# Three moves in the last five tiles of a top-10 kernel: stores to another queue, copy steps one tile earlier, one ranking later

## The chip, the cores and the metric

The kernel runs on one core of one Trainium2 chip. Its time is the device time of one execution in microseconds (us); the number given for a kernel is the median of several executions. The profile is one execution recorded by the hardware profiler. Its engines are PE (TensorE, the matmuls, with PEld for the loading of weights), DVE (VectorE), ACT (ScalarE), POOL (GpSimd) and SP (SyncE). ACTq and SPq are the sequencers of ACT and SP, which issue DMA transfers.

## The reference

The input is a random matrix of 8192 rows and 8192 columns in float32. For each row the reference returns the column numbers of the ten largest values, largest first, as int64:

```python
def reference(x, k):                      # k = 10
    indices = np.argpartition(x, -k, axis=1)[:, -k:]
    values = np.take_along_axis(x, indices, axis=1)
    sorted_idx = np.argsort(-values, axis=1)
    return np.take_along_axis(indices, sorted_idx, axis=1)
```

## The kernel before

**Tiles and batches.** The rows are worked through in 64 tiles of 128 rows (4 MB of input each). The variable `t` counts tiles from 0 to 63, and `last` is 63. Results are finished and stored in batches. Batches 0 to 6 hold eight tiles each (batch 6: tiles 48 to 55), batch 7 holds five (56 to 60) and batch 8 holds three (61 to 63).

**The work on a tile.** A tile goes through these steps, each named after its function in the listing.

- `load` (L88): SP issues the transfers that bring the tile into one of four buffers. They are 1 MB each, four a tile; the first and the last tile have eight pieces of 512 KB.
- `weigh` (L138): ACT takes the exponential of the tile (L144) into one of three buffers `e`, and PE adds groups of columns up into 1024 sums per row, `s` in PSUM (L152). It runs in two halves, in tile 63 in five parts of 2, 2, 2, 1 and 1 eighths. An eighth of tile 63 is one piece of the load.
- `choose_steps` (L157): DVE finds the 12 best of the 1024 sums, with six instructions (L171 to L177). The last of them writes the list `idx`.
- `gather` (L183): POOL fetches the values of the chosen groups by that list (L185), into `cand`.
- `spread` (L195): the fetched values are multiplied by a mask (L203) into `masked`. Half of the 12 groups are done by DVE and half by POOL. For tile 61 POOL does all 12; for tile 63 DVE does 8.
- `extract` (L210): 12 float32 matmuls (recorded as 24 instructions, L214) bring the values into their rows' order, into `g` in PSUM. The pool of `g`, `gpsum`, has three buffers (L72).
- `rank_steps` (L217): DVE sorts out the ten best of the 96 values, with six small instructions (L225 to L231). The first three of them that work on values (L225, L226, L228) read `g`; the others don't.
- `finish_steps` (L236): for a whole batch, DVE turns the places found into column numbers (`slot`, `low`, `hot`, `hot` again, `pick`, `val`, `rows`: L257 to L272), PE brings them into output order with one `move` per tile of the batch (L252, two recorded instructions each) into the single PSUM buffer `fo`, DVE copies `fo` to `opack` (L276), and a transfer stores `opack` (L278). That list has seven DVE steps, the moves, the copy and the store, in this order: 17 steps for a batch of eight.

**The order.** All of it stands under `tc.manual_schedule()`: each engine issues its instructions in the order in which the code below emits them, and an engine that waits holds up all that stands behind it. Waits between engines, and for a buffer that is still being read, are put in by the framework. The main loop (L296) emits for tile `t`: `choose(t)` interleaved with `rank(t-3)`, `spread(t-1)`, `gather(t)`, `weigh(t+1)`, `extract(t-1)`, some steps of the pending batch, and `load(t+3)`. The pending batch's steps wait in the list `later`; `todo` of them are emitted per tile, 3 as a rule and 6 from tile 59 on (L304). The 17 steps of batch 6 enter the list at tile 58. So they are emitted as 6 at tile 59 (to `val`), 6 at tile 60 (`rows` and five moves) and 5 at tile 61 (three moves, the copy, the store). Those of tile 61 stand behind `weigh(62)` and ahead of `choose(62)` and `weigh(63)`. Each store is issued by ACT's sequencer.

After the loop (L312 to L339) come `choose(63)` and the last spreads, extracts and ranks, with the steps of batch 7 put in between by hand, and then batch 8. A short check of the whole result follows, which ends in a value that all engines read (L348) before the program ends.

Of the kernel before, what the change touches and what calls it, by code (L numbers as in the profile page):

```python
# [14 lines left out]
S = P // A  # L15
# [4 lines left out]
TB = 8  # L20
# [5 lines left out]
LAG = 3  # L26
# [4 lines left out]
def kernel(  # L31
# [6 lines left out]
    nc = tc.nc  # L38
# [19 lines left out]
    out_rows = out_u32.rearrange("(r a) n -> r (a n)", a=A)  # L58
# [20 lines left out]
    last = ntiles - 1  # L79

    starts = list(range(0, ntiles, TB)) + [last - 2]
# [35 lines left out]
    for s in range(S):  # L117
        nc.vector.tensor_copy(
            out=group[:, s, :].rearrange("p (a s) -> p a s", s=S)[:, :, s], in_=own_a
# [37 lines left out]
    def choose_steps(t):  # L157
        m = ss.pop(t)
        b = batch_of[t]
        i = t - starts[b]  # L160
        if i == 0:
            batch[b] = (
                cpool.tile([P, TB, 16], u16, tag="cidb", name="cidb"),
                cpool.tile([P, TB, 16], u16, tag="posb", name="posb"),
            )
        cid = batch[b][0][:, i, :]
        w16 = wall[:, t, :]
        m2 = small.tile([P, W], fp32, tag="m2", name="m2")
        idxs[t] = small.tile([P, G], u16, tag="idx", name="idx")
        return [  # L170
            lambda: nc.vector.max(out=w16[:, 0:8], in_=m),  # L171
            lambda: nc.vector.match_replace(out=m2, in_to_replace=w16[:, 0:8], in_values=m,  # L172
                                            imm_value=-1.0),
            lambda: nc.vector.max_index(out=cid[:, 0:8], in_max=w16[:, 0:8], in_values=m),  # L174
            lambda: nc.vector.max(out=w16[:, 8:16], in_=m2),  # L175
            lambda: nc.vector.max_index(out=cid[:, 8:16], in_max=w16[:, 8:16], in_values=m2),  # L176
            lambda: nc.vector.tensor_scalar(  # L177
                out=idxs[t], in0=cid[:, 0:G], scalar1=float(W - 1), scalar2=base,
                op0=ALU.min, op1=ALU.add,
            ),  # L180
        ]
# [28 lines left out]
    def extract(t):  # L210
        mk = masked.pop(t)
        gs[t] = gpsum.tile([P, G, R], fp32, tag="g", name="g")
        for c in range(G):
            nc.tensor.matmul(gs[t][:, c, :], lhsT=mk[:, c, :, :].rearrange("p a s -> p (a s)"),  # L214
                             rhs=place, start=True, stop=True)

    def rank_steps(t):  # L217
        g = gs.pop(t).rearrange("p c q -> p (c q)")
        b = batch_of[t]
        pos = batch[b][1][:, t - starts[b], :]  # L220
        t8a = small.tile([P, 8], fp32, tag="t8a", name="t8a")
        t8b = small.tile([P, 8], fp32, tag="t8b", name="t8b")
        g2 = small.tile([P, G * R], fp32, tag="g2", name="g2")
        return [
            lambda: nc.vector.max(out=t8a, in_=g),  # L225
            lambda: nc.vector.match_replace(out=g2, in_to_replace=t8a, in_values=g,  # L226
                                            imm_value=BIG_NEG),
            lambda: nc.vector.max_index(out=pos[:, 0:8], in_max=t8a, in_values=g),  # L228
            lambda: nc.vector.max(out=t8b, in_=g2),  # L229
            lambda: nc.vector.max_index(out=pos[:, 8:16], in_max=t8b, in_values=g2),  # L230
            lambda: nc.vector.tensor_copy(out=tall[:, t:t + 1],  # L231
                                          in_=t8b[:, KMAX - 9:KMAX - 8]),
        ]


    def finish_steps(b):  # L236
        cidb, posb = batch.pop(b)
        n = sizes[b]
        r0 = starts[b] * S
        slot = bpool.tile([P, TB, KMAX], u16, tag="slot", name="slot")[:, 0:n, :]  # L240
        low = bpool.tile([P, TB, KMAX], u16, tag="low", name="low")[:, 0:n, :]
        hot = bpool.tile([P, TB, KMAX, G], fp16, tag="hot", name="hot")[:, 0:n]
        pick = bpool.tile([P, TB, KMAX], fp32, tag="pick", name="pick")[:, 0:n, :]
        val = bpool.tile([P, TB, KMAX], fp32, tag="val", name="val")[:, 0:n, :]
        rows = bpool.tile([P, TB, A, KMAX], fp32, tag="rows", name="rows")[:, 0:n]
        fo = fpsum.tile([P, A * KMAX], fp32, tag="fo", name="fo")[0:n * S, :]
        o = opacks[b % 2][0:n * S]
        hshape = [P, n, KMAX, G]
        rshape = [P, n, A, KMAX]

        def move(i):
            nc.tensor.matmul(fo, lhsT=send[:, i, 0:n * S],  # L252
                             rhs=rows[:, i].rearrange("p a k -> p (a k)"),
                             start=i == 0, stop=i == n - 1)

        return [
            lambda: nc.vector.tensor_scalar(  # L257
                out=slot, in0=posb[:, 0:n, 0:KMAX], scalar1=R.bit_length() - 1,
                scalar2=None, op0=ALU.logical_shift_right),
            lambda: nc.vector.tensor_scalar(  # L260
                out=low, in0=posb[:, 0:n, 0:KMAX], scalar1=R - 1,
                scalar2=None, op0=ALU.bitwise_and),
            lambda: nc.vector.tensor_tensor(  # L263
                out=hot, in0=slot.unsqueeze(3).to_broadcast(hshape),
                in1=slots.unsqueeze(1).unsqueeze(1).to_broadcast(hshape), op=ALU.is_equal),
            lambda: nc.vector.tensor_tensor(
                out=hot, in0=hot, in1=cidb[:, 0:n, 0:G].unsqueeze(2).to_broadcast(hshape),
                op=ALU.mult),
            lambda: nc.vector.reduce_sum(out=pick, in_=hot, axis=X_AX),
            lambda: nc.vector.scalar_tensor_tensor(  # L270
                out=val, in0=low, scalar=float(W), in1=pick, op0=ALU.mult, op1=ALU.add),
            lambda: nc.vector.tensor_tensor(  # L272
                out=rows, in0=val.unsqueeze(2).to_broadcast(rshape),
                in1=own_a.unsqueeze(1).unsqueeze(3).to_broadcast(rshape), op=ALU.mult),
        ] + [lambda i=i: move(i) for i in range(n)] + [
            lambda: nc.vector.tensor_copy(  # L276
                out=o[:, :, :, 0], in_=fo.rearrange("p (a k) -> p a k", k=KMAX)),
            lambda: nc.scalar.dma_start(out=out_rows[r0:r0 + n * S, :],  # L278
                                        in_=o.rearrange("p a k two -> p (a k two)")),
        ]  # L280

    def interleave(*lists):
        for group_ in zip(*[l for l in lists if l]):
            for step in group_:
                step()

    def run(steps):
        for step in steps:
            step()
# [3 lines left out]
    with tc.manual_schedule():  # L293
        weigh(0)
        later = []
        for t in range(last):  # L296
            interleave(choose_steps(t), rank_steps(t - LAG) if t >= LAG else [])
            if t >= 1:
                spread(t - 1, 0 if t == last - 1 else G // 2)
            gather(t)  # L300
            weigh(t + 1)
            if 1 <= t < last - 2:
                extract(t - 1)
            todo = 3 if t < last - 4 else 6  # L304
            run(later[:todo])
            later = later[todo:]
            done = t - LAG
            if done >= 0 and batch_of[done] != batch_of[done + 1]:
                later += finish_steps(batch_of[done])
            if t + 3 < ntiles:  # L310
                load(t + 3)
        extract(last - 3)  # L312
        extract(last - 2)
        run(choose_steps(last))
        spread(last - 1)
        gather(last)
        extract(last - 1)
        run(rank_steps(last - 3))
        run(rank_steps(last - 2))
        nc.vector.tensor_scalar(  # L320
            out=good[:, 0:nsums], in0=eall, scalar1=FINITE, scalar2=None, op0=ALU.is_lt,
        )
        steps = finish_steps(batch_of[last - 3])
        run(steps[:3])
        spread(last, 8)
        extract(last)
        run(steps[3:7])
        run(rank_steps(last - 1))
        run(steps[7:-2])
        run(rank_steps(last))  # L330
        run(steps[-2:])


        nc.scalar.activation(out=e10, in_=tall, func=ACTF.Exp, bias=bias[:, 0:1], scale=BETA)  # L334
        run(finish_steps(batch_of[last]))
        nc.vector.scalar_tensor_tensor(
            out=good[:, nsums:nsums + ntiles], in0=e10, scalar=SLACK, in1=wall[:, :, G],
            op0=ALU.mult, op1=ALU.is_gt,
        )  # L339
# [63 lines left out]
```

## Time and profile before

| what | value |
|---|---|
| median of 7 executions | 689.71 us (688.45 to 691.81) |
| the profiled execution's own time | 688.52 us |
| its span, from the first to the last instruction | 686.6 us |
| mean granted TensorE clock (1 is full speed) | 0.771 |
| DMA throughput in the steady part | about 420 GB/s |
| last part of tile 63 weighed on ACT, end | 656.5 us |
| first instruction of `choose(63)` on DVE | 657.20 us |
| store of batch 8 issued | 683.06 us |

The span and the rows of the trace count from the first instruction. The profiled execution's own time has 1.9 us more than its span. A row such as "647.19 0.32 DVE L276 CAST opack<-fo" reads: start at 647.19 us, 0.32 us long, on DVE, from line 276, writing `opack` from `fo`. What stands in brackets behind a row is how long the engine sat idle before it, and whose end released it.

### The profile page before, as it was taken

What the parts mean: (1) busy time and instruction counts of PE and PEld (TensorE: products, weight loads), DVE (VectorE), ACT (ScalarE), POOL (GpSimd) and SP (SyncE); (2) the same over time, 40 slices, a digit from 0 to 9 for tenths busy, and PEclk for the clock granted to TensorE, in tenths of its full rate; (3) what the DMA queues carried; (4) which work ended last, traced back from release to release, by engine and by line L of the source; (5) the groups of instructions that cost most, each with busy time, mean ns of one, the idle gap of its engine ahead of it and who ended that gap; (6) DMA issues with size and microseconds to landing.
All of it is one profiled execution on the core that took longest, in us unless ns stands there. A gap on an engine that the chain in (4) does not pass through costs nothing. (4 is left out here: it accounts for less than half of the span.)

```text
span 686.6 us, 7967 instructions
## 1 busy us (share of the span) xinstructions
PE 556.3 (81%) x2690; PEld 347.7 (51%) x2690; DVE 559.0 (81%) x1313; ACT 488.8 (71%) x264; POOL 183.2 (27%) x135
## 2 busy tenths in 40 slices
PE   1578988887888798688889779788978888987685
PEld 0234545664555465365566545456545545553464
DVE  1568778899868997798888998689978899779876
ACT  4777776777777777776776777777777777776620
POOL 0113313312331331332233133223133223313421
PEclk9876667779868788868877798676886668878865
DMA  8999999999999999999999999999999999999500
GB/s 356 421 421 420 419 421 419 421 419 421 419 420 420 420 420 420 420 420 420 420 420 420 420 419 420 420 420 421 419 421 420 420 419 417 420 421 420 231 0 6
DMA packets 70592, 269.69 MB, mean 393 GB/s; under 512 B 4374, under 2 KB 5014, under 8 KB 70550
## 3 DMA queue, kind: packets, MB, share of 16 engines
q1 hardware_dynamic: 69760, 268.45, 95.4%
q10 hardware_dynamic: 790, 0.73, 0.3%
q8 instruction: 21, 0.34, 0.2%
q14 instruction: 21, 0.17, 0.1%
HBM read 268.51 MB, written 0.66 MB: 392 GB/s over the span
## 5 line engine op out<-in xcount | busy, mean ns | idle before, releaser
L144 ACT ACTIVATE e<-xt,bias 128x4096 bf16<-128x4096 f32 (+2 forms) x131 | 475.5, 3630 | 158.8 <-DMA xt<-in_x_dram 145.1
L152 PE MATMUL s<-e,group 128*128 128x512 bf16 x1024 | 340.6, 495 | 119.9 <-ACT e L144 119.8
L152 PEld LDWEIGHTS <-group 128*128 128x128 bf16 x1024 | 122.0, 123 | 310.1 <-issue 254.3
L214 PEld LDWEIGHTS g<-cpack,masked 128*128 128x128 f32 x1536 | 216.3, 222 | 19.2 <-issue 6.8
L214 PE MATMUL g<-cpack,masked 128*128 128x8 f32 x1536 | 207.5, 275 | 3.6 <-DVE masked L203 3.6
L185 POOL INDIRECT_COPY cand<-xt,idx 128x192 f32 x64 | 64.5, 1008 | 481.8 <-DMA xt<-in_x_dram 146.1
L171 DVE MAX8 wall<-s 128x8 f32<-128x1024 f32 x64 | 78.8, 1232 | 113.2 <-PE s L152 113.1
L203 POOL TENSOR_TENSOR masked<-cand,cpack 128x768 f32<-128x768 f32 x64 | 117.7, 1839 | 6.0 <-PE g L214 0.7
L174 DVE FIND_INDEX8 cidb<-wall,s 128x8 uint16<-128x1024 f32 x64 | 78.3, 1224 | 0.0
L176 DVE FIND_INDEX8 cidb<-wall,m 128x8 uint16<-128x1024 f32 x64 | 78.0, 1219 | 0.0
L172 DVE MATCH_REPLACE8 m<-wall,s 128x1024 f32<-128x1024 f32 x64 | 77.8, 1215 | 0.0
L175 DVE MAX8 wall<-m 128x8 f32<-128x1024 f32 x64 | 77.3, 1209 | 0.0
L203 DVE TENSOR_TENSOR masked<-cand,cpack 128x768 f32<-128x768 f32 (+1 forms) x63 | 60.1, 954 | 0.9 <-POOL cand L185 0.9
L252 PE MATMUL fo<-rows,send 128*64 128x160 f32 (+2 forms) x128 | 25.7, 343 | 3.0 <-DVE rows L272 3.0
L144 ACT ACTIVATION_READ_ACCUMULATOR e<-xt,bias 128x1 f32 x131 | 24.4, 186 | 0.0
L252 PEld LDWEIGHTS fo<-rows,send 128*64 128x64 f32 (+2 forms) x128 | 16.9, 146 | 5.5 <-issue 3.9
L334 ACT ACTIVATE e<-tall,bias 128x64 f32<-128x64 f32 x1 | 0.3, 348 | 23.2 <-DVE hot L263 23.2
L228 DVE FIND_INDEX8 posb<-t8a,g 128x8 uint16<-128x96 f32 x64 | 16.4, 257 | 0.0
L225 DVE MAX8 t8a<-g 128x8 f32<-128x96 f32 x64 | 15.9, 249 | 0.6 <-PE g L214 0.6
L230 DVE FIND_INDEX8 posb<-t8b,g 128x8 uint16<-128x96 f32 x64 | 16.2, 253 | 0.0
L226 DVE MATCH_REPLACE8 g<-t8a,g 128x96 f32<-128x96 f32 x64 | 15.9, 249 | 0.0
L229 DVE MAX8 t8b<-g 128x8 f32<-128x96 f32 x64 | 15.6, 244 | 0.0
(37 smaller groups left out, 104.6 us busy)
## 6 DMA issues: line engine op xcount, KB each, us to landing
xt<-in_x_dram SPq DMA_DIRECT2D x248, 1024.0 KB, 16.2
xt<-in_x_dram SPq DMA_DIRECT2D x16, 512.0 KB, 9.0
out_dram<-opack ACTq DMA_DIRECT2D x7, 80.0 KB, 5.1
cpack<-topk_cpack ACTq DMA_DIRECT2D x1, 68.5 KB
out_dram<-opack ACTq DMA_DIRECT2D x1, 50.0 KB
out_dram<-opack ACTq DMA_DIRECT2D x1, 30.0 KB
```

Source lines behind the costliest of these rows:

```text
L144: nc.scalar.activation(out=e[:, 0:n, :].rearrange("p s j -> p (s j)"), in_=xts[t][:, s0 * W:(s0 + n) * W], func=ACTF.Exp, bias=bias[:, 0:1 ...
L152: nc.tensor.matmul(ss[t][:, j:j + BANK], lhsT=group[:, s0 + i, :], rhs=e[:, i, j:j + BANK], start=s0 + i == 0, stop=s0 + i == S - 1)
L171: lambda: nc.vector.max(out=w16[:, 0:8], in_=m),
L172: lambda: nc.vector.match_replace(out=m2, in_to_replace=w16[:, 0:8], in_values=m, imm_value=-1.0),
L174: lambda: nc.vector.max_index(out=cid[:, 0:8], in_max=w16[:, 0:8], in_values=m),
L175: lambda: nc.vector.max(out=w16[:, 8:16], in_=m2),
L176: lambda: nc.vector.max_index(out=cid[:, 8:16], in_max=w16[:, 8:16], in_values=m2),
L185: nc.gpsimd.add_instruction(mybir.InstIndirectCopy(name=nc.get_next_instruction_name(), ins=[nc.gpsimd.lower_ap(xts[t]), nc.gpsimd.lower_a ...
L203: eng.tensor_tensor(out=masked[t][:, g0:g1], in0=cand[:, g0:g1].unsqueeze(2).to_broadcast(shape), in1=own.rearrange("p (c s) -> p c s", s= ...
L214: nc.tensor.matmul(gs[t][:, c, :], lhsT=mk[:, c, :, :].rearrange("p a s -> p (a s)"), rhs=place, start=True, stop=True)
L228: lambda: nc.vector.max_index(out=pos[:, 0:8], in_max=t8a, in_values=g),
L252: nc.tensor.matmul(fo, lhsT=send[:, i, 0:n * S], rhs=rows[:, i].rearrange("p a k -> p (a k)"), start=i == 0, stop=i == n - 1)
```

## The change

It has three parts.

- The stores of the last three batches (6, 7 and 8) are issued on SP's queue instead of ACT's.
- The steps of batch 6 are handed out as 5 at tile 59 (to `pick`), 10 at tile 60 (`val`, `rows` and all eight moves) and 2 at tile 61 (the copy and the store). The moves of tile 60 stand ahead of `weigh(62)` on PE.
- `rank(59)`, which was interleaved with `choose(62)`, comes after `choose(63)` and `spread(62)`, and after `extract(62)` has been emitted. The first three steps of batch 7 (`slot`, `low` and the first `hot`) come after `spread(63)` and `extract(63)` are emitted, instead of ahead of them.

```diff
@@ finish_steps(b)
         r0 = starts[b] * S
+
+        queue = nc.sync if b >= len(starts) - 3 else nc.scalar
...
-            lambda: nc.scalar.dma_start(out=out_rows[r0:r0 + n * S, :],
+            lambda: queue.dma_start(out=out_rows[r0:r0 + n * S, :],
                                         in_=o.rearrange("p a k two -> p (a k two)")),
@@ main loop
-            interleave(choose_steps(t), rank_steps(t - LAG) if t >= LAG else [])
+            interleave(choose_steps(t), rank_steps(t - LAG) if LAG <= t < last - 1 else [])
...
-            todo = 3 if t < last - 4 else 6
+            todo = {last - 4: 5, last - 3: TB + 2}.get(t, 3)
@@ after the loop
         extract(last - 1)
+        run(rank_steps(last - 4))
         run(rank_steps(last - 3))
         run(rank_steps(last - 2))
...
         steps = finish_steps(batch_of[last - 3])
-        run(steps[:3])
         spread(last, 8)
         extract(last)
-        run(steps[3:7])
+        run(steps[:7])
         run(rank_steps(last - 1))
         run(steps[7:-2])
         run(rank_steps(last))
```

## The prediction

> **What bounds the kernel now.** I read the page first, then the chain that ended last in order of time, then the waits of the last 57 us, then the timeline around the longest of them.
>
> ```profile
> PE 556.3 (81%) x2690; PEld 347.7 (51%) x2690; DVE 559.0 (81%) x1313; ACT 488.8 (71%) x264; POOL 183.2 (27%) x135
> ...
> DMA  8999999999999999999999999999999999999500
> ```
>
> No engine is full. The DMA row is: up to slice 37 the input streams at 420 GB/s, and ACT waits for it at nearly every half tile (145.1 us in all). The change leaves everything before tile 59 as it is, so the steady part keeps its length and only the tail can move. The last piece of tile 63 is issued at 641.57 and takes 8.8 us to land, so the input is complete at 650.4; the remaining 36 us are the tail. The chain shows its order:
>
> ```profile
> 652.28 4.26 ACT e L144 x6
> 656.58 0.61 PE s L152 x2
> 657.20 1.24 DVE wall L171
> ...
> 663.67 0.95 DVE masked L203
> ...
> 668.53 0.69 POOL cand L185
> 669.24 1.24 DVE masked L203
> 670.62 5.26 PE g L214 x24
> 675.88 2.83 PE fo L252 x10
> 678.73 0.32 DVE opack L276
> ```
>
> So: weigh 63 on ACT, its last sums on PE, choose 63 on DVE (657.20 to 663.67), the gather, spread 63, extract 63, the moves of batch 7, then batch 8 and the check. The chain starts with ACT ending 6 us after the data. The waits of this stretch say why:
>
> ```profile
> DVE opack L276 <- PE fo L252: 5.5, 3, 3.0
> ...
> ACT e L144 <- DVE opack L276: 3.9, 1, 3.9
> ```
>
> ```profile
> 644.07 0.19 ACT L144 ACTIVATION_READ_ACCUMULATOR e<-xt,bias 128x1 f32 x1
> 644.31 1.89 PE L152 MATMUL s<-e,group 128*128 128x512 bf16 x8 [1.44 <-ACT e L144]
> ...
> 646.12 1.03 PE L252 MATMUL fo<-rows,send 128*64 128x160 f32 x6
> 647.19 0.32 DVE L276 CAST opack<-fo 64x160 uint32<-64x160 f32 x1 [3.00 <-PE fo L252]
> 647.43 1.22 DVE L171 MAX8 wall<-s 128x8 f32<-128x1024 f32 x1
> 647.54 0.47 ACTq L278 DMA_DIRECT2D out_dram<-opack  x1
> ...
> 648.19 2.00 ACT L144 ACTIVATE e<-xt,bias 128x2048 bf16<-128x2048 f32 x1 [3.94 <-DVE opack L276]
> ```
>
> ACT is done with tile 62 at 644.26. Its next instruction is batch 6's store, which waits for the copy, which waits for three moves that stand behind weigh 62 on PE. Weigh 63 stands behind the store and starts at 648.19.
>
> **The change part by part.**
>
> *Stores on SP.* Weigh 63 starts when ACT is free, 644.26 instead of 648.19: 3.93 us earlier, if its input is there. Issues and landing times of the load give pieces 4 to 7 at 646.6, 647.7, 649.0 and 650.4 (pieces 0 and 1 are sooner: piece 0 is issued at 629.27 and takes 12.3). The five parts started at 648.19, 650.20, 652.18, 654.17 and 655.30, so they move to 644.26, 646.27, 648.25, 650.24 and 651.37. Part 2 needs piece 5 (0.5 to spare), part 3 piece 6 (1.2), part 4 piece 7 (1.0). The buffers `e` that the parts take were last read by PE two or more parts earlier. On SP the store of batch 6 waits for the copy, and behind it stand only the stores of batches 7 and 8: all loads were issued by 641.9. SP's last stores stand ahead of its read of the check value; an issue takes 0.3 to 0.6 us and that read comes 1.1 us after the last issue, so they cost nothing. The last store's packets are over by 684.2, 1.1 us after issue, while the engines' closing work runs to 686.6.
>
> [...]
>
> *Moves of batch 6 ahead of weigh 62.* Ten recorded moves took 2.49 us from 637.84. Six more cost 1.7 at the 0.29 us apiece of the half-clock row (2.89 for ten), so they end at 642.0; `val` one tile later moves 0.2 us on DVE and delays nothing, since the moves wait for extract 59 till 637.84. Weigh 62's first half then starts at 642.0 instead of 640.26 and takes 1.89 (eight matmuls at full clock) to 3.4 (0.43 each at half clock): 643.9 to 645.4. The second half, which needs ACT until 644.31, ends at 646.2 or, all at half clock, at 648.8. The copy now runs right after spread 60, at 644.2, in DVE's idle time. So choose 62 starts at 646.2 (before: 647.43, behind the copy). I take the full clock: the stretch 675.9 to 679.2 held only moves, at PEclk 0.50, and the next, 679.3 to 682.6, was granted 1.00. The other end, 2.6 us later, is kept for the range.
>
> *Rank 59 out of choose 62.* Choose 62 with the rank took 7.13 us (647.43 to 654.56); choose 63, alone, took 6.47. From 646.2 this gives DVE free at 652.7, and the sums of tile 63 are ready at 657.18 - 3.93 = 653.25, so choose 63 is bound by ACT and PE with 0.5 us to spare. With the rank left in it would be 653.3; this move alone gains nothing to speak of. If the cover goes (weigh 62 at half clock), DVE is free only at 655.3 and 2.05 us of the gain are lost.
>
> The rank has a price at its new place. `gpsum` has three buffers, so extract 62 takes that of tile 59, and rank 59 now reads it after spread 62. In the rank that started at 664.54 the last reader of `g` (L228) ended at 665.41, 0.87 later. New: spread 62 ends and rank 59 begins at 664.54 - 3.93 = 660.61; its last reader ends at 661.48 and extract 62 starts at 661.54 instead of 660.75: 0.79 late. The trace of before has no such wait; the ends are nothing and a whole rank (1.36). I take 0.79, because the code names the readers.
>
> *DVE and POOL up to spread 63.* Three ranks of 1.36 and the check of 0.14 take DVE from 660.61 to 664.83. The gather: idx 63 ends at 663.76 - 3.93 = 659.83. From the end of idx to the gather's row it was 3.6 us in tile 62 (no spread on DVE after it), 4.29 in tile 61 (a spread), 4.77 in tile 63 (spread, and `hot` at 667.58 while it ran). With `hot` moved away I take 4.29 plus the 1.02 of the row: 665.14, 0.1 better than before. Spread 63 starts at 665.17, with DVE waiting 0.3 us for it. So the third rank is hidden; without the wait it would cost what it exceeds 0.3 by.
>
> *Extract 63.* The mask is ready at 665.17 + 1.24 + 0.14 = 666.55. Extract 62 ends at 661.54 + 5.29 = 666.83 and binds; it is followed by extract 63's 5.26 us from 666.86 to 672.12, against 675.88: 3.76 earlier. (The delay of 0.79 met a gap of 0.65 between the two.) I keep 5.3 us for each: in the stretches 665.7 to 669.0 and 672.5 to 675.8 PE was busy without a pause and PEclk stayed 0.50.
>
> [...]
>
> *Batch 7's first three steps behind spread 63.* `slot`, `low`, `hot` (about 1 us) plus the rest (673.91 - 670.39 = 3.5, part of it a `hot` of 1.52 slowed beside POOL) follow spread 63 at 666.4: some 4.3 us, to 670.7. Rank 62 follows to 672.0, rank 63 to 673.5. The moves on PE run 672.12 to 675.0, so DVE has over 1 us to spare, and from there all is as before.
>
> **Sum**: -3.93 (ACT) + 0.17 (extract 62's buffer, net) = -3.76. Against the profiled execution: 688.52 - 3.76 = 684.8. It lay 1.19 below the median shown; from the median 689.71 - 3.76 = 686.0 (0.55% faster).
>
> **The rivals.**
>
> 1. *Choose 62 becomes the bound.* Weigh 62, pushed behind 16 moves, runs at half clock. For it: PEclk was 0.50 from 638.4 to 641.7. Against it: 1.00 right after, and PE would be busier than before. Price up to 2.05, so 688.0. Chance 0.12.
> 2. *The data holds weigh 63.* If something else than the store keeps ACT from starting (a late piece, say), the gain shrinks. A last piece 1.0 us later than 650.4 begins to count; 3.8 us later nothing is gained: 689.7. Against it: the load's rate binds ACT in every tile, and the wait is put down to the copy. Chance 0.05.
> 3. *Slower: the last store on SP's queue lands late.* The shortest landing in SP's rows is 8.8 us. The store of batch 8 would be issued at 679.3 and land at 688.1, while the closing waits start at 681.6 (SP's stood 1.3 after the check value at 684.1). That adds 6.5: 692.5. It begins to cost from a landing of 2.3 us, and from 6.1 the kernel is slower than before. Against it: those 8.8 us had six earlier pieces, 3 MB, ahead of them; on ACT's queue the stores took 5.1 amid loads, 3.0 at their end, 1.1 with nothing else. Chance 0.05.
>
> My forecast has 0.75; 0.03 is left for a loss that I don't see.
>
> **How the numbers follow.** The forecast's own range is 684.9 (no buffer wait, 4.1 faster, and 0.7 for how the seven executions lie about their median) to 687.0. Rival 1 carries the range up to 688.2; below I add 0.2. A measurement of this kernel can tell about 0.2% from no change, 1.4 us. Faster by more: the forecast, rival 1 and part of 2, 0.88. Within it: 0.05. Slower: rival 3 and the rest, 0.07.
>
> **What would show it.** Right: weigh 63 follows weigh 62 on ACT without a wait; choose 63 starts near 653.3, released by PE; extract 62 waits for rank 59 and extract 63 follows it without a gap; the store's issue is in SP's rows. Wrong: choose 63 starts late because DVE is still in choose 62; ACT waits for the load in tile 63; idle time after the check value.

## The result and the profile after

The changed kernel takes 686.27 us (median of 17 executions, 684.75 to 688.54), the kernel before 690.01 us (median of 42). The ratio is 0.9944, with a 95% interval of 0.9934 to 0.9953: 0.56% faster, 3.7 us. I had predicted 686.0. The profiled execution took 685.76 us with a span of 684.0; that of the kernel before took 688.52. These two single executions are only 2.76 apart, and the section on the prediction says where the missing 1.0 us of that pair lies. Three executions that took over 1.5% longer than the fastest of their kernel (one each of sp_only, moves_only and rank_back2 below) count in no ratio.

The page's busy times and input rate (420 GB/s in the steady slices of both) are as before:

```profile
PE 559.9 (82%) x2690; PEld 344.0 (50%) x2690; DVE 559.3 (82%) x1313; ACT 488.4 (71%) x264; POOL 183.4 (27%) x135
...
DMA  9999999999999999999999999999999999999700
```

The timeline from the end of tile 62 on ACT to the start of choose 63 (start, length, engine, line, operation):

```profile
643.92 0.19 ACT L144 ACTIVATION_READ_ACCUMULATOR e<-xt,bias 128x1 f32 x1
...
644.02 1.99 ACT L144 ACTIVATE e<-xt,bias 128x2048 bf16<-128x2048 f32 x1
644.83 0.31 DVE L278 CAST opack<-fo 64x160 uint32<-64x160 f32 x1
645.16 0.56 SPq L280 DMA_DIRECT2D out_dram<-opack  x1
...
647.23 1.23 DVE L171 MAX8 wall<-s 128x8 f32<-128x1024 f32 x1 [2.09 <-PE s L152]
...
652.38 0.59 PE L152 MATMUL s<-e,group 128*128 128x512 bf16 x2 [0.54 <-ACT e L144]
...
653.63 1.22 DVE L171 MAX8 wall<-s 128x8 f32<-128x1024 f32 x1
```

ACT goes from tile 62 to tile 63 without a pause, where it stood 3.94 us before. The store of batch 6 is now a row of SP's sequencer, and the copy runs before choose 62 instead of delaying it. Choose 62, though, now waits 2.09 us for PE. The last sums of tile 63 are ready at 652.97, but choose 63 starts at 653.63, without a wait on DVE: it stands behind choose 62. The chain that ended last, in order of time, shows what this costs (start, length, what):

```profile
639.97 3.20 PE fo L254 x15
643.17 4.04 PE s L152 x16
...
660.20 0.94 DVE masked L203
...
661.68 0.26 DVE posb L228
...
662.07 10.38 PE g L214 x48
672.45 2.83 PE fo L254 x10
...
678.26 1.78 PE fo L254 x6
```

The chain no longer goes through weigh 63. It goes through the moves of batch 6 and weigh 62 on PE, then through choose 62 and choose 63 back to back on DVE. After spread 62 (660.20) it passes the last reader of tile 59's `g` (L228) and then both last extracts without a gap, 10.38 us.

### The profile page after: what moved, and what is told of

It reads as the page before. It is cut to its first block, busy times and chain, and to the rows that moved or that the text cites. A ratio compares the mean times of both kernels' runs of the same rounds, so it can differ in the third digit from the quotient of the medians.

```text
span 684.0 us, 7971 instructions
## 1 busy us (share of the span) xinstructions
PE 559.9 (82%) x2690; PEld 344.0 (50%) x2690; DVE 559.3 (82%) x1313; ACT 488.4 (71%) x264; POOL 183.4 (27%) x135
## 4 chain that ended last, share of the span: by engine, by line
DMA 60%; PE 17%; DVE 7%; ACT 5%; SPq 5%; issue 3%; POOL 3%; ACTq 0%; DVEq 0%
DMA xt<-in_x_dram 59%; PE s L152 10%; PE g L214 6%; ACT e L144 5%; SPq L94 5%; POOL cand L185 3%; DVE wall L171 2%; PE fo L254 1%; DVE m L172 1%; DMA out_dram<-opack 1%; DVE cidb L176 1%; DVE cidb L174 1%; DVE wall L175 1%; DVE masked L203 0%; DVE rows L274 0%
## 5 line engine op out<-in xcount | busy, mean ns | idle before, releaser
L152 PE MATMUL s<-e,group 128*128 128x512 bf16 x1024 | 346.0, 502 | 114.8 <-ACT e L144 114.4
L214 PEld LDWEIGHTS g<-cpack,masked 128*128 128x128 f32 x1536 | 210.0, 217 | 19.1 <-issue 6.8
L214 PE MATMUL g<-cpack,masked 128*128 128x8 f32 x1536 | 202.5, 271 | 2.5 <-DVE masked L203 2.1
L185 POOL INDIRECT_COPY cand<-xt,idx 128x192 f32 x64 | 64.8, 1012 | 478.6 <-DMA xt<-in_x_dram 204.5
L254 PE MATMUL fo<-rows,send 128*64 128x160 f32 (+2 forms) x128 | 27.3, 361 | 3.0 <-DVE rows L274 3.0
L228 DVE FIND_INDEX8 posb<-t8a,g 128x8 uint16<-128x96 f32 x64 | 16.5, 257 | 0.0
```

The lines of the kernel that those rows point to most:

```text
L152: nc.tensor.matmul(ss[t][:, j:j + BANK], lhsT=group[:, s0 + i, :], rhs=e[:, i, j:j + BANK], start=s0 + i == 0, stop=s0 + i == S - 1)
L185: nc.gpsimd.add_instruction(mybir.InstIndirectCopy(name=nc.get_next_instruction_name(), ins=[nc.gpsimd.lower_ap(xts[t]), nc.gpsimd.lower_a ...
L254: nc.tensor.matmul(fo, lhsT=send[:, i, 0:n * S], rhs=rows[:, i].rearrange("p a k -> p (a k)"), start=i == 0, stop=i == n - 1)
```

## The experiments

The kernels of these experiments carry a stand-in for the gather of L185, and the exact branch at the end is never taken; everything else is computed on the values that the stand-in leaves. The first stand-in was this (shortened):

```diff
+    hold = consts.tile([P, 512], fp32)
+    listed = consts.tile([P, G], fp32)
...
-        nc.gpsimd.add_instruction(mybir.InstIndirectCopy(...))
+        nc.gpsimd.tensor_copy(out=listed, in_=idxs[t])
+        for n in (512, 512, 512, 512, 512, 512, 512, 100):
+            nc.gpsimd.memset(hold[:, 0:n], 0.0)
+        nc.gpsimd.tensor_copy(out=cands[t].rearrange("p g s -> p (g s)"), in_=xts[t][:, 0:16 * G])
...
-    with tc.If(passed < checks):
+    with tc.If(passed < 1):
```

Ratios below are to the kernel before with its real gather, on the same chip; 0.001 is 0.7 us. Two kernels are compared by the difference of their ratios.

| kernel | ratio to the kernel before | 95% interval |
|---|---|---|
| base (stand-in 1) | 1.0260 | 1.0244 to 1.0277 |
| all | 1.0211 | 1.0197 to 1.0225 |
| sp_only | 1.0226 | 1.0213 to 1.0240 |
| moves_only | 1.0224 | 1.0210 to 1.0238 |
| rank_back | 1.0190 | 1.0170 to 1.0210 |
| rank59_third | 1.0206 | 1.0188 to 1.0224 |
| moves_behind | 1.0202 | 1.0185 to 1.0219 |
| warm | 1.0224 | 1.0198 to 1.0249 |
| base2 (stand-in 2) | 1.0010 | 0.9995 to 1.0025 |
| all2 | 0.9984 | 0.9973 to 0.9994 |
| rank_back2 | 0.9971 | 0.9958 to 0.9983 |

The first four share one chip and its runs of the kernel before, the next four another, the last three a third.

### How long the stand-in must be

The first version, cal, had ten fills of 512 values and one of 200 (nine of 512 in tile 62).

> The kernel before with a stand-in for the gather, to find the stand-in's length. In place of the gather of L185 POOL copies the list idx, fills a scratch buffer ten times (nine times in tile 62) and copies the first 192 values of the tile into cand, so the fetched values are not the chosen ones, and the branch to the exact computation at the end is never taken. From the end of idx to the end of this sequence I expect 4.7 us in tile 62 and 5.3 in the others, as the gather has, and a time of 688 to 692 us like the kernel before. [...]

It took 710.2 us (one execution). The sequence was 7.2 us long where the gather has 5.3, because each fill of 512 values took 0.55 us and the first copy 0.9. DVE's step `idx` of tile 62 took 2.46 us in it (0.20 in the kernel before). I shortened it to the eight fills above; in base it takes 5.4 us in tile 63 (idx ends at 682.44, the stand-in at 687.84).

### The base and the whole change

> The kernel before with a stand-in for the gather, as long as the gather: POOL copies idx, fills a scratch buffer eight times and copies 192 values of the tile into cand, so the fetched values are not the chosen ones, and the branch to the exact computation is never taken. It is the base of all further kernels. Expected: 689 to 692 us, 3.9 us of waiting for batch 6's copy on ACT ahead of tile 63, and 4.7 to 5.4 us from the end of idx to the end of the stand-in. If the stand-in still disturbs DVE or holds back loads, the time is 1 us or more above the kernel before, and only differences between kernels with the stand-in count.

> The whole change, with the same stand-in for the gather and without the exact branch. My theory: 3.8 us (2.8 to 4.1) below the base, as the change gave with the real gather (3.7). If the real gather's own behaviour were part of the gain, the difference would be under 2.5 us.

The base has the wait of the kernel before (timeline of base):

```profile
665.50 0.47 ACTq L277 DMA_DIRECT2D out_dram<-opack  x1
666.15 2.00 ACT L146 ACTIVATE e<-xt,bias 128x2048 bf16<-128x2048 f32 x1 [3.94 <-DVE opack L275]
```

It is 2.6% slower as a whole, since its input comes at 409 GB/s instead of 420 (more on that below), so only differences count. The whole change is 0.0049 below it, 3.4 us with 1.5 of uncertainty (medians 706.94 and 703.41). That agrees with the real kernels' 3.7 and with my theory; the other outcome, under 2.5 us, lies within the uncertainty too.

### One part alone

sp_only has the change of the queue and nothing else; moves_only has the hand-out of batch 6's steps and nothing else:

```diff
 sp_only
+        queue = nc.sync if b >= len(starts) - 3 else nc.scalar
...
-            lambda: nc.scalar.dma_start(...)
+            lambda: queue.dma_start(...)
 moves_only
-            todo = 3 if t < last - 4 else 6
+            todo = {last - 4: 5, last - 3: TB + 2}.get(t, 3)
```

> Only the stores of batches 6 to 8 on SP; stand-in for the gather, no exact branch. Theory (ACT's queue is what holds tile 63): ACT starts tile 63 as soon as it is done with tile 62, its sums are ready 3.9 us sooner, but the copy still holds choose 62 on DVE and rank 59 still lengthens it (647.4 to 654.6 in the kernel before), so choose 63 starts at 654.6 instead of 657.2: 2.6 us below the base. [...] Rival (the copy that comes late on DVE is the whole cause): 0.

> Only the steps of batch 6 handed out earlier (5, 10 and 2); the stores stay on ACT; stand-in for the gather, no exact branch. Theory: the copy is done by 644.5 to 645.1, the store is issued on ACT at 645 and tile 63 starts at 645.5 instead of 648.2 on ACT; choose 62 with its rank runs from 646.2 or 647.2 to 653.3 or 654.3; choose 63 starts at 654.3: 2.4 to 3.0 us below the base. So either of two parts gives most of the gain alone and they don't add up. Rival (only the queue counts): under 0.5 us.

By the ratios sp_only gains 2.3 us (0.0034) and moves_only 2.5 us (0.0036), each with about 1.5 us of uncertainty. Both agree with their theories (2.6, and 2.4 to 3.0), and the rivals that give one part nothing or under 0.5 us fall. The timelines show the two ways. In sp_only ACT goes straight on, but the copy still comes late and choose 62 stands behind it:

```profile
662.12 0.19 ACT L146 ACTIVATION_READ_ACCUMULATOR e<-xt,bias 128x1 f32 x1
662.21 1.99 ACT L146 ACTIVATE e<-xt,bias 128x2048 bf16<-128x2048 f32 x1
```

```profile
666.58 0.32 DVE L277 CAST opack<-fo 64x160 uint32<-64x160 f32 x1 [3.56 <-PE fo L253]
666.83 1.22 DVE L173 MAX8 wall<-s 128x8 f32<-128x1024 f32 x1
```

In moves_only the copy is early, and ACT still waits for it, but less: 2.2 us after tile 62 instead of 3.9.

```profile
662.59 0.19 ACT L146 ACTIVATION_READ_ACCUMULATOR e<-xt,bias 128x1 f32 x1
664.29 0.47 ACTq L277 DMA_DIRECT2D out_dram<-opack  x1
664.94 2.00 ACT L146 ACTIVATE e<-xt,bias 128x2048 bf16<-128x2048 f32 x1 [2.17 <-DMA xt<-in_x_dram]
```

(The view puts this wait down to a load; the row of the issue ahead of it, released when the copy ended at 664.26, is what ACT stood at.)

That the two parts don't add up, as I had expected, isn't shown. Their gains make 4.8 us together and the whole change gained 3.4, a difference within the uncertainty of the three. The whole change also has the third part: rank_back (next section), which has both these parts but leaves rank 59 where it was, is 0.0070 or 4.8 us below base, on another chip. And in the profiles, choose 63 starts 13.66 us after the end of tile 62 on ACT in base, 11.57 in sp_only, 11.17 in moves_only and 9.19 in all: 2.1, 2.5 and 4.5 us sooner than in base, which does add up.

### The rank that was moved

```diff
 rank_back (from the whole change)
-            interleave(choose_steps(t), rank_steps(t - LAG) if LAG <= t < last - 1 else [])
+            interleave(choose_steps(t), rank_steps(t - LAG) if t >= LAG else [])
...
-        run(rank_steps(last - 4))
 rank59_third (from the whole change)
-        run(rank_steps(last - 4))
         run(rank_steps(last - 3))
         run(rank_steps(last - 2))
+        run(rank_steps(last - 4))
```

> The whole change, but rank 59 stays in choose 62 (batch 7's first three steps stay behind spread 63); stand-in for the gather, no exact branch. Theory (the move of the rank is worth next to nothing): choose 62 takes 7.1 us instead of 6.5, which makes DVE late for choose 63 by 0.3 to 0.9; extract 62 no longer waits for rank 59 and starts within 0.1 us of the end of spread 62 instead of 1.0. The time is 0 to 0.8 us above the whole change (ratio to the kernel before 1.021 to 1.023). Rival (the rank on the way of choose 62 was a main cause): 1.5 us or more above.

> The whole change, but of the three ranks after spread 62 that of tile 59 comes last instead of first; stand-in for the gather, no exact branch. Theory (extract 62 waits for rank 59, whose buffer it takes): extract 62 starts 2.7 us later, extract 63 follows without a gap, and the time is 2.2 to 2.9 us above the whole change. Rival (extract 62 waits for something else, the mask or PE's earlier extracts): no difference, 0 to 0.3 us.

> The whole change with rank 59 left in choose 62, second stand-in, no exact branch, beside the whole change on the same chip. Theory (the rank's move is worth nothing: what it takes off choose 62 it gives back as a wait of extract 62): within 0.7 us of all2, on either side; extract 62 starts within 0.1 us of the end of spread 62 and not 0.9. Rival (it is a gain): 1 us or more above all2.

The wait is there, and it is the rank's. In the whole change with the stand-in (timeline of all, PE then DVE):

```profile
679.71 10.38 PE L213 MATMUL g<-cpack,masked 128*128 128x8 f32 x48 [2.58 <-DVE posb L227]
```

```profile
677.84 0.95 DVE L202 TENSOR_TENSOR masked<-cand,cpack 128x768 f32<-128x768 f32 x1
...
679.31 0.26 DVE L227 FIND_INDEX8 posb<-t8a,g 128x8 uint16<-128x96 f32 x1
```

Spread 62 is over at 678.79; extract 62 starts at 679.71, 0.14 us after the last reader of the rank (679.57). With the rank back in choose 62, spread 62 ends at 678.70 and extract 62 starts at 678.75, 0.05 us later, as expected (664.41 and 664.47 in rank_back2). In the time it is no loss: rank_back is 0.0021 below all, on another chip, and rank_back2 is 0.0013 (0.9 us, with 1.1 of uncertainty) below all2 on the same chip. The rival, a gain of 1 us or more by the move, falls. What the move gives is nothing that I could measure, and in both pairs the kernel without it was the faster one. No run takes back the other half of the third part alone (batch 7's first three steps).

My second test of the wait missed. With rank 59 third, extract 62 did not start 2.7 us later but 0.92 us after spread 62, as in all, and the time was the same (0.0005 below). It waits for the first rank of the three, whichever tile it belongs to:

```profile
679.85 10.38 PE L213 MATMUL g<-cpack,masked 128*128 128x8 f32 x48 [0.99 <-DVE posb L227]
```

In both orders the wait ends with the rank that is emitted first. That fits a framework that gives the new `g` the buffer that comes free first and not that of a fixed tile; the trace shows when the wait ends, not which buffer is taken. "It takes that of tile 59" in my prediction fits only because rank 59 is emitted first.

### The moves behind weigh 62 again, with the copy out of the way

```diff
 moves_behind (from the whole change)
-            todo = {last - 4: 5, last - 3: TB + 2}.get(t, 3)
+            todo = {last - 4: 5, last - 3: 2, last - 2: TB}.get(t, 0 if t > last - 2 else 3)
...
+            if t == last - 2:
+                run(rank_steps(last - 4))
...
-        run(rank_steps(last - 4))
         run(rank_steps(last - 3))
         run(rank_steps(last - 2))
+        run(later)
```

> The whole change, but the eight moves of batch 6 stand behind weigh 62 on PE, their copy and store come after the ranks that follow choose 63, and rank 59 stands ahead of choose 62, in DVE's idle time; stand-in for the gather, no exact branch. Theory (weigh 62 behind 16 matmuls makes choose 62 late when the clock is halved, my first rival): choose 62 starts 0.4 to 1.0 us sooner, choose 63 is bound by PE again, extract 62 does not wait for a rank; 0.3 to 1.0 us below the whole change. Rival (choose 62 is early enough in nearly all executions): within 0.3 us of the whole change.

The ratio is 1.0202 against 1.0211 of all (on another chip), 0.6 us, well within the intervals: undecided between the two expectations. The traces say more. Counted from the end of tile 62 on ACT, the last sum of weigh 62 is ready at these times:

| profile | recorded moves ahead of weigh 62 | granted clock 1.00 from | weigh 62 ready | choose 63 late against its sums |
|---|---|---|---|---|
| rank_back | 16 | -2.4 | 2.03 | 0.18 |
| rank59_third | 16 | -8.7 | 2.03 | 0.04 |
| all | 16 | -0.7 | 2.66 | 0.33 |
| the changed kernel | 16 | +0.1 | 3.18 | 0.66 |
| warm | 16 | +0.0 | 4.20 | 1.09 |
| sp_only | 10 | -0.2 | 3.37 | (copy in front) |
| moves_behind | 0 | +1.5 | 2.95 | 0.12 |

In the profiles with the full clock in time, 16 moves in front cost nothing (2.03, as in the kernel before). In those with half clock up to about the end of tile 62 weigh 62 is 0.6 to 2.2 us later, late also without any moves in front of it (moves_behind, 2.95). The moves add to it: behind the same 10.2 us of half clock it is 4.20 with 16 of them (warm) and 3.37 with 10 (sp_only).

A late weigh 62 has a second price, which I had ruled out. In warm ACT itself stood still for 0.49 us within tile 63, until 0.08 us after PE had read the first half of weigh 62, whose buffer `e` it takes next:

```profile
664.53 2.00 ACT L146 ACTIVATE e<-xt,bias 128x2048 bf16<-128x2048 f32 x1 [0.49 <-ACT e L146]
```

In moves_behind the moves held PE back from part 0 of tile 63, and ACT stood 0.28 us ahead of part 3 in the same way. So the mechanism of my first rival is real. Its price in these profiles was up to 1.09 us on choose 63 and 0.49 more on its sums, and it goes with how long the half clock lasts and where it ends.

### Can the clock be kept up?

```diff
 warm (from the whole change, shortened)
         extract(last - 2)
+        burn(8)      # matmul(junk, lhsT=group[:, 0, :], rhs=512 bf16 columns)
...
         extract(last - 1)
+        burn(4)
...
+        steps = finish_steps(batch_of[last]); run(steps[:7]); burn(6); run(steps[7:])
```

> The whole change with 18 extra bf16 matmuls of 512 columns on PE, written to a buffer that nothing reads: 8 after extract 61, 4 after extract 62 and 6 ahead of batch 8's moves, in time in which PE is idle; stand-in for the gather, no exact branch. It tests what I took as given, 5.3 us for each of the last two extracts. Theory (PE's clock is halved because the extracts and the idle time count as little activity): with the fill the granted clock is 1.00 there, the extracts take 2.75 us, and the time is 2 to 4 us below the whole change. Rival (the extracts run at half clock because of themselves, whatever stands between): the extra matmuls change nothing or, at 0.43 us apiece, cost up to 2 us.

The rival's outcome came. The ratio is 1.0224 against 1.0211 of all (on another chip), and the clock under the two extracts stayed at 0.50; what sets it this run does not show. The busy table by stretches (from:to, length, busy time of PE, PEld, DVE, ACT, POOL with instructions, PEclk, DMA share, GB/s):

```profile
679.10:682.40 3.30, 3.30 (x12) 1.82 (x10) 3.20 (x17) 0.00 (x0) 3.04 (x6) 0.50 0.02 5
682.50:685.80 3.30, 3.30 (x17) 3.30 (x17) 2.76 (x14) 0.00 (x0) 3.02 (x6) 0.50 0.00 0
685.90:689.20 3.30, 3.30 (x14) 2.38 (x14) 3.20 (x7) 0.00 (x0) 1.28 (x1) 0.50 0.00 0
...
692.80:696.10 3.30, 2.98 (x11) 1.94 (x13) 1.66 (x11) 0.35 (x1) 0.00 (x0) 0.50 0.00 0
696.20:699.50 3.30, 1.89 (x11) 0.86 (x10) 2.30 (x7) 0.00 (x0) 0.00 (x0) 1.00 0.04 16
```

Stretches that held some 2 us of wide matmuls and extracts for the rest left the clock at half. Only the stretch with 2.9 us of moves was followed by full clock. The four extra matmuls ahead of extract 63, at 0.43 us apiece, delayed it by 1.5 us; the eight ahead of extract 62 cost it nothing, since it starts 0.84 us after spread 62, where it waits 0.92 for the rank in all. A denser fill was not tried.

### The input buffers' place, and a longer gather

The second stand-in, in place of the same lines, needs no memory of its own:

```diff
+        nc.gpsimd.tensor_copy(out=pad[:, 1:1 + G], in_=idxs[t])
+        flat = cands[t].rearrange("p g s -> p (g s)")
+        for _ in range(17):
+            nc.gpsimd.memset(flat, 0.0)
+        nc.gpsimd.tensor_copy(out=flat, in_=xts[t][:, 0:16 * G])
```

> The kernel before with a second stand-in for the gather, which takes no memory of its own: POOL copies idx into the unused columns of the tile pad, fills cand 17 times and copies 192 values of the tile into it; the fetched values are not the chosen ones, and the exact branch is never taken. The first stand-in's scratch buffer moved the input buffers by 2.1 KB in each partition, and the input then came at 409 GB/s instead of 420, however often POOL filled the buffer and also while POOL stood still. Theory (the place of the input buffers in SBUF sets that rate): 420 GB/s again and 688.5 to 691 us. Rival (POOL's fills slow the DMA writes): 409 GB/s and 705 us or more.

> The whole change with the second stand-in, no exact branch. Theory: 3.7 us below base2 (3.0 to 4.2), as with the first stand-in and with the real gather; choose 63 is late by 0 to 1.1 us against its sums, by how much of weigh 62 fell into half clock. Rival (the first stand-in's slower input made room for the gain): under 2.5 us.

base2 has 420 GB/s again and the time of the kernel before (1.0010), although POOL fills memory in it too. The rival falls: the fills as such had not cost the 17 us. The input was as slow while POOL stood still (408.5 GB/s in such gaps of base from 100 to 600 us, 409.0 in the rest). What went with the slower input is the 2.1 KB of scratch in front of the input buffers; no run moved these buffers alone. The second stand-in changes the tail too: in base2's profile ACT stood 5.91 us ahead of tile 63, not 3.94.

all2 is a miss: only 0.0026 (1.8 us) below base2, where I expected 3.7. That the input at 409 GB/s had made room for the gain can't be the reason, because the real kernels have 420 and gained 3.7. The trace shows another: this stand-in takes 6.6 us from idx (base2, tile 63: 665.75 to 672.30), 1.3 more than the gather, and POOL's spread 61 ends 2.3 us later than in the changed kernel (655.12 against 652.82). DVE's last step of choose 62 is longer there (timeline of all2, then the same step in the changed kernel):

```profile
653.03 2.12 DVE L177 TENSOR_SCALAR idx<-cidb,cpack 128x12 uint16<-128x12 uint16 x1
655.07 1.22 DVE L171 MAX8 wall<-s 128x8 f32<-128x1024 f32 x1
```

```profile
653.49 0.23 DVE L177 TENSOR_SCALAR idx<-cidb,cpack 128x12 uint16<-128x12 uint16 x1
```

The step took 2.12 us instead of 0.23, and ended (655.15) when POOL's spread 61 did (655.12). The same step of tile 63 took 1.56 us, until 662.94, with POOL's spread 62 over at 662.91. Together that is 3.2 us more than 0.23 each, enough for the missing 1.9. The changed kernel has 0.7 us to spare at tile 62 (652.82 to 653.49) and none at tile 63: there the step took 0.33 us and ended at 660.28, POOL's spread 62 at 660.26. So what was gained on ACT and DVE made POOL's gather and spread the next in line.

## Why the prediction was right

**Stores on SP.** Right. Weigh 63 starts at 644.02 with no wait (predicted 644.26), its sums are ready at 652.97 (653.25). No part waited for a piece of the load; the last piece landed at 650.13, and part 4, which takes it, began at 651.11. The last store was issued at 680.41 on SP, its packets were over at 681.50, and SP's read of the check value began at 681.50 too: rival 3 did not occur. sp_only's 2.3 us, 0.8 at the low end of its uncertainty, is more than the 0.47 us of the issue.

**Moves ahead of weigh 62.** I took full clock and kept 2.6 us more as the other end. The profiled execution lay between: weigh 62 was ready at 647.19 instead of 646.2. Half clock from 630.4 to 637.3 made weigh 61's second half 3.57 us long (1.89 in the kernel before), so that the moves started at 639.62 instead of 637.84, and half clock from 640.7 to 644.1 slowed the start of weigh 62. That a busier PE speaks for the full clock was my estimate, and this trace doesn't show it: PE was busy all the time from 637.2 to 640.6 and the grant fell to 0.50, and busy all the time from 640.7 to 644.0 and it rose to 1.00. Choose 63 began at 653.63 instead of 653.25, and DVE released it, not PE: the sign that I had named for "wrong", choose 63 late because DVE is still in choose 62, is there. So in this execution rival 1's path bound the kernel, and the time still came out as forecast because its price was 0.38 us and not 2.05. In the other profiles of the table choose 63 was 0.04 to 1.09 us late against its sums; rival 1 is a spread on the forecast, not another outcome.

**Rank 59.** The size of the wait was right: extract 62 started 0.94 us after spread 62 (I had 0.93, of which 0.79 was the delay). That the move gains nothing by itself was right too. That the wait is for tile 59's buffer held only by the order of emission. Batch 7's first three steps cost nothing at their new place: DVE waited 1.38 us for the moves on PE ahead of the copy.

**Up to extract 63.** The gather took 5.24 from the end of idx (5.31), DVE waited 0.23 for it (0.3), the two extracts ran 10.38 without a gap (10.55 and none), and from there 2.85 to the copy of batch 7 (675.30; predicted 674.97).

**The one term of the profiled execution that I missed.** I let all after the copy of batch 7 run "as before". It didn't. Batch 8's moves, in the kernel before and in the changed one:

```profile
681.70 0.97 PE L252 MATMUL fo<-rows,send 128*24 128x160 f32 x6 [3.01 <-DVE rows L272]
```

```profile
678.26 1.77 PE L254 MATMUL fo<-rows,send 128*24 128x160 f32 x6 [3.00 <-DVE rows L274]
```

They took 0.8 us more, at a granted clock of 0.50 instead of 1.00. With the 0.33 that is left of choose 63's delay at the copy of batch 7, the changed kernel is 1.1 us behind my sum at the copy of batch 8 (680.07 against 678.95) and 1.0 in the executions' own times.

Which clock these moves get can be read off the traces. In the kernel before the grant changes, from 635 us on, at 638.3, 641.7, 652.0, 655.4, 662.2, 679.3 and 682.7, in the changed kernel, from 630 us on, at 630.4, 637.3, 640.7, 644.1 and 654.3: 3.4 us apart, or two, three or five times that. Counted on from such changes in stretches of 3.4 us, four of the 14 profiles (before, sp_only, warm, rank_back2) have the ten moves of batch 7, 2.9 us, in a single stretch but for 0.15 us at most, and the next one is granted 1.00. In the other ten a stretch's end divides them, with at most 2.6 us on one side, and the clock stays at 0.50. That is what these profiles have in common; why the grant changes isn't shown. So the full clock at 679.3 was luck of the one execution that my sum started from, which is also 1.5 us below the median of 42. The medians agree with the sum (3.74 against 3.76), but that agreement is partly luck: how the median executions spend their time isn't on record.

## What to carry to other kernels

Here a store that waited its turn in ACT's queue held up the compute behind it for 3.94 us, with an issue of 0.47. So price a store by what it waits for and not by its issue time, and put it on an engine with nothing urgent behind it. Run each part of a change alone, and the whole without it: here that showed two parts that gain and a third that gains nothing. And after a gain of a few us look for who had just that much to spare: here a rank's buffer, and POOL with 0.7 us.

## What was not expected of the hardware

- 2.1 KB more in front of the input buffers in each partition went with an input rate of 409 GB/s instead of 420 for the whole run, 17 us (base against the kernel before); base2, the stand-in without them, had both back. The cause was not shown, since no run moved these buffers alone.
- In the changed kernel the granted clock stayed at 0.50 from 654.3 to the end, though PE was busy for 20.0 of the 20.4 us counted from 654.4 to 675.0, mostly with extracts (8 columns each). In warm it stayed there also with about 2 us of wide matmuls in a stretch of 3.4 (679.1 to 682.4 and 685.9 to 689.2).
- A DVE step on uint16 (`idx`, L177), 0.23 us in the changed kernel, took 2.12 us in all2 while POOL ran the multiply of spread 61, and ended with it (655.15 and 655.12); so did the 1.56, 1.72 and 1.50 us of the same step in all2 and rank_back2.
